# An encoder block on one core: four transposes move between the first products, attention scores start one step sooner, pooling uses four banks, and the operands of the last product lie at other addresses

## The chip, the core and the metric

The kernel runs on one core of a Trainium2 chip. The metric is the device time of one execution in microseconds. Five engines work in parallel, each in its own program order: TensorE (PE in the profile; its weight loads are PEld), VectorE (DVE), ScalarE (ACT), GpSimd (POOL) and SyncE (SP, which only issues transfers). Engines wait for one another through semaphores. Products accumulate in PSUM banks; everything else lies in SBUF, 128 partitions wide.

## The reference

```python
h = rmsnorm(x) * norm_gain
z = h @ w_in                     # 256 x 1024 by 1024 x 8192
a_in, a_gate, q, k, v, b_gp, g_logits = split(z)
y_a = (pooled_means(a_in) @ w_pool * pool_scale * silu(a_gate)) @ w_proj_a
att = dilated_attention(q, k, v) # 3 groups x 8 heads of 64, biased, masked;
                                 # the groups share one softmax denominator
y_b = (att * silu(b_gp)) @ w_proj_b
merged = sigmoid(gA) * y_a + sigmoid(gB) * y_b
return rmsnorm(x + merged @ w_out) * final_gain
```

There are 256 tokens, two blocks of 128. `pooled_means` takes centred means over 2, 4, 8 and 16 tokens, minus the token.

## The kernel before

**Three products for one.** Each float32 operand is split into a rounded high part and the rest. A product is then three matmuls, high by high, high by low and low by high, which `mm3` records (L249, L250, L251). `hh` and `hl` are the parts of the normalised input, `whi` and `wlo` those of a weight tile. One half of a weight tile, 128 output channels by 256 tokens, is 8 x 3 = 24 matmuls of 256 columns.

**The head** (to 16 us) is ordered by hand, in `manual_schedule`, on ACT, DVE, PE and POOL. X is squared, summed and scaled into `XN`, one token block b at a time; DVE scales channels 0 to 511 and ACT channels 512 to 1023 (L196, L197). `turn(kc, b)` (L206) transposes channel block kc of token block b on PE into `tps[kc % 4]`: four PSUM banks, each holding channel blocks kc and kc + 4. ACT reads a turned block into `hh` (L225), and DVE makes `hl` from it (L226). `part0(kc, x)` (L215) records two products of the first weight tile: x = 0 is high by high, x = 1 takes `hl`, x = 2 takes `wlo`. DVE copies the first weight tile into `whi0` in two halves (L199), and POOL computes its low part (`cut_lo`, L165). Three small products for the bias lines (L239) stand between the x = 2 products.

**The stages** that follow are ordered by a scheduler from the program's text. They work through weight tiles: k, q and v of the first four head pairs (I = 0), then u, a and b (pool input and the two gates), then v, k and q of I = 1, then eight gate tiles g with the pooling product mx before the eighth, then the two projections y, and at last the product with `w_out`, whose accumulators are called both and out. While tile n is multiplied, tile n + 2 is split (`cut_half`, L129 on ACT, L134 on DVE).

**Attention items.** An item is a head pair hq and a token block b. `stage_s` makes its scores (four matmuls, sp, L294 and L296), DVE adds the bias and finds the row maximum (L297, L303), ACT exponentiates (L306). `stage_t` turns the result (pt, L318) and splits it (L320, L321). `stage_o` multiplies with v (op, L332 and L335); after the second token block of a pair, ACT and DVE add the result into `ATT` (L346 to L348). There is one score bank pair ("S") and one op bank ("O"). `step()` is called after every half tile. It records at most one op, one turning and one new score; an item is turned two steps after its scores, and multiplied two steps after that. `due` grows by `rate` at each step, and a new item starts when it passes 0.99.

**Addresses.** `skip(nbytes, name)` allocates a tile that nobody uses and so moves what is allocated after it. `MH` and `ML`, the parts of the merged result, take the places of the bias tile ("bias") and of the keys ("kl").

**Projection banks.** Accumulators of half tiles rotate through three banks ("mm").

Of the kernel before, what the change touches and what calls it, by code (L numbers as in the profile page):

```python
# [12 lines left out]
F32R = mybir.dt.float32r  # L13
# [4 lines left out]
P = 128  # L18
D = 1024
S = 256  # L20
KC = D // P
# [21 lines left out]
def encoder_block(ctx: ExitStack, tc: tile.TileContext, x, w_in, lines, w_pool, w_proj_a, w_proj_b,  # L43
                  w_out, final_gain, params, out):
    nc = tc.nc
# [7 lines left out]
    def slot(shape, dt, tag, name, bufs=1):  # L53
        return sb.tile(shape, dt, tag=tag, name=name, bufs=bufs)

    def skip(nbytes, name):

        if nbytes:
            sb.tile([P, nbytes // 4], F32, name=name)

    def bank(shape, tag, name, bufs):
        return ps.tile(shape, F32, tag=tag, name=name, bufs=bufs)

    def mmb(name, shape=(P, S)):
        return bank(list(shape), "mm", name, 3)
# [97 lines left out]
    def cut_lo(n, k0, k1, eng):  # L163
        t, (hi, lo) = raws[n][0], parts[n]
        return eng.tensor_tensor(lo[:, k0:k1, :], t[:, k0:k1, :], hi[:, k0:k1, :].bitcast(F32), op=ALU.subtract)  # L165
# [6 lines left out]
    with tc.manual_schedule(engines={mybir.EngineType.Activation, mybir.EngineType.DVE, mybir.EngineType.PE,  # L172
                                    mybir.EngineType.Pool}):
        tiny = sb.tile([P, 1], F32, name="tiny")
        warm = sb.tile([P, P], F32, name="warm")
        nc.vector.memset(warm, 0.0)
        nc.scalar.activation(tiny, warm[:, 0:1], AF.Square)

        def keep_warm(times):
            for _ in range(times):  # L180
                nc.tensor.matmul(misc[:, P:2 * P], warm, warm, start=True, stop=True)

        keep_warm(WARM)
        halves = [slice(h * 512, (h + 1) * 512) for h in range(2)]
        for b in range(2):
            sq = [slot([P, 512], F32, "st", f"sq{b}{h}", 3) for h in range(2)]
            nc.scalar.activation(sq[0], X[:, b, halves[0]], AF.Square, scale=1.0 / 32.0, accum_out=ss[:, b, 0:1])
            xb = X[:, b, halves[1]]
            nc.vector.tensor_tensor_reduce(sq[1], xb, xb, scale=1.0 / D, scalar=EPS, op0=ALU.mult, op1=ALU.add,
                                           accum_out=ss[:, b, 1:2])  # L190
            t = slot([P, 1], F32, "rt", f"rt{b}", 2)
            nc.vector.tensor_tensor(t, ss[:, b, 0:1], ss[:, b, 1:2], op=ALU.add)
            nc.gpsimd.tensor_tensor(rs[:, b:b + 1], t, mhalf, op=ALU.pow)
        open_parts(0)
        for b in range(2):
            nc.vector.tensor_scalar(XN[:, b, halves[0]], X[:, b, halves[0]], rs[:, b:b + 1], None, op0=ALU.mult)  # L196
            nc.scalar.activation(XN[:, b, halves[1]], X[:, b, halves[1]], AF.Copy, scale=rs[:, b:b + 1])  # L197
        for k in (0, 4):
            nc.vector.tensor_copy(parts[0][0][:, k:k + 4, :], raws[0][0][:, k:k + 4, :])  # L199

        cut_lo(0, 0, 5, nc.gpsimd)
        first_lo = cut_lo(0, 5, 8, nc.gpsimd)
        tps = [bank([P, 2, S], "mm" if i < 3 else "T", f"tp{i}", 3 if i < 3 else 2) for i in range(4)]

        def turn(kc, b):
            nc.tensor.transpose(tps[kc % 4][:, kc // 4, b * P:(b + 1) * P], XN[:, b, kc * P:(kc + 1) * P], ident)  # L206

        acc = bank([P, 2, 512], "S", "k00", 1)
        acc0 = [acc[:, u, 0:S] for u in range(2)]

        def part0(kc, x):
            hi_, lo_ = parts[0]
            for u in range(2):
                c = slice(u * P, (u + 1) * P)
                nc.tensor.matmul(acc0[u], (lo_ if x == 2 else hi_)[:, kc, c], (hl if x == 1 else hh)[:, kc, :],  # L215
                                 start=x == 0 and kc == 0, stop=x == 2 and kc == KC - 1)

        for kc in range(KC):
            turn(kc, 0)
        for kc in range(KC):  # L220
            turn(kc // 2 + kc % 2 * 4, 1)
        for kc in range(KC):
            v = tps[kc % 4][:, kc // 4]
            gcol = prm[:, kc:kc + 1]
            nc.scalar.activation(hh[:, kc, :], v, AF.Copy, scale=gcol)  # L225
            nc.vector.scalar_tensor_tensor(hl[:, kc, :], v, gcol, hh[:, kc, :].bitcast(F32), op0=ALU.mult,  # L226
                                           op1=ALU.subtract)
            part0(kc, 0)
            if kc >= 2:
                part0(kc - 2, 1)  # L230
        for kc in (6, 7):
            part0(kc, 1)
        for kc in range(KC):
            if kc == 5:

                for t in range(3):
                    w = 3 * NH
                    o = 3 * P + t // 2 * w
                    nc.tensor.matmul(misc[:, t * w:(t + 1) * w], oh[:, t * P:(t + 1) * P], oh[:, o:o + w],  # L239
                                     start=True, stop=True)  # L240
            part0(kc, 2)
        cut_next()
        nc.vector.tensor_copy(line.rearrange("p i r h -> p r i h"),
                              misc[:, 0:LROW * NH].rearrange("p (r i h) -> p r i h", i=2, h=4))
        cut_next()
    parts.pop(0)

    def mm3(acc, ah, al, bh, bl, first, last):
        nc.tensor.matmul(acc, ah, bh, start=first, stop=False)  # L249
        nc.tensor.matmul(acc, ah, bl, start=False, stop=False)  # L250
        nc.tensor.matmul(acc, al, bh, start=False, stop=last)  # L251
# [101 lines left out]
    due, rate = [1.0 - RATES[0]], [RATES[0]]  # L353

    def step():
        clock[0] += 1
        for it in live:
            if it["at"] == "t" and it["when"] <= clock[0]:
                stage_o(*it["it"], it["p"])
                it["at"] = "done"  # L360
                break
        live[:] = [it for it in live if it["at"] != "done"]
        for it in live:
            if it["at"] == "s" and it["when"] <= clock[0]:
                it["p"] = stage_t(*it["it"], it["st"])
                it["at"], it["when"] = "t", clock[0] + LAG_O
                break
        due[0] = due[0] + rate[0] if wait else due[0]
        if wait and due[0] > 0.99:
            due[0] -= 1.0  # L370
            it = wait.pop(0)
            live.append({"it": it, "at": "s", "when": clock[0] + LAG_T, "st": stage_s(*it)})
# [95 lines left out]
    def bias(I):  # L468
        T = skew.pop(I)
        t = slot([P, S + 4 * 640], F32, "bias", f"BT{I}")  # L470
        BL[I], BT[I] = t[:, 0:S], t[:, S:].rearrange("p (h c) -> p h c", c=640)
        by = T.rearrange("p c a h -> p h a c")
        for h in range(4):
            nc.gpsimd.tensor_copy(BT[I][:, h, 0:384].rearrange("p (a c) -> p a c", c=64), by[:, h, 0:6])
        for rl in range(2):
            rows = slice(rl * 64, (rl + 1) * 64)
            for g in range(2):
                o = 384 + g * P + 64 * (rl if g == 0 else 1 - rl)
                nc.gpsimd.tensor_copy(BT[I][rows, :, o:o + 64], by[rows, :, 6 + g + rl])
                o = 384 + g * P + 64 * (1 - rl if g == 0 else rl)  # L480
                behind(nc.gpsimd.memset(BT[I][rows, :, o:o + 64], MASK), first_lo)
# [6 lines left out]
    heads(0, "k")  # L488

    heads(0, "q")  # L490
    bias(0)
    U = sb.tile([P, 4, UW], F32, tag="uu", name="U")
    nc.gpsimd.memset(U[:, :, 0:PAD], 0.0)
    nc.gpsimd.memset(U[:, :, PAD + S:], 0.0)
    heads(0, "v")
    skip(608, "pt")
    wait += [(0, hq, b) for hq in range(4) for b in range(2)]


    for dst in ("u", "a", "b"):  # L500
# [15 lines left out]
    for g, w in enumerate(POOL_W):  # L516
        h = w // 2
        cur, lo_, n_ = U[:, g, :], 0, UW
        k = 1
# [36 lines left out]
    heads(1, "q")  # L556
    bias(1)
    rate[0] = RATES[1]
    due[0] = 1.0 - rate[0]
    wait += [(1, hq, b) for hq in range(4) for b in range(2)]  # L560


# [32 lines left out]
    AML = slot([P, 4, S], F32R, "t4", "AML")  # L595
    wph, wpl = weights(n)
    n += 1
    for g in range(4):
        acc = mmb(f"mx{g}") if g < 3 else bank([P, 2, 512], "S", "mx3", 1)[:, 0, 0:S]
        mm3(acc, wph[:, g, :], wpl[:, g, :], PH[:, g, :], PL[:, g, :], True, True)  # L600
        am = AM[:, g, :].rearrange("p (r j) -> p r j", r=4)
        nc.vector.scalar_tensor_tensor(am, acc.rearrange("p (j r) -> p r j", r=4), prm[:, 24 + g:25 + g],
                                       SA[:, g, :].rearrange("p (r j) -> p r j", r=4), op0=ALU.mult,
                                       op1=ALU.mult)
# [47 lines left out]
    squash((GG[:, 8:12], G2))  # L652

    MH = slot([P, 8, S], F32R, "bias", "MH")
    ML = slot([P, 8 * S + 32], F32R, "kl", "ML")[:, 32:].rearrange("p (c j) -> p c j", j=S)

    def done_b(cb, acc):
        nc.vector.tensor_tensor(GB[cb], acc, GB[cb], op=ALU.mult)
# [183 lines left out]
```

## Time and profile before

| | |
|---|---|
| time, median of 3 runs | 260.26 us (259.99 to 260.36) |
| the profiled execution | 260.05 us, of which the span from first to last instruction is 258.3 us |
| granted TensorE clock, mean | 0.993 |
| PE busy | 250.5 us, 97% of the span |
| DVE, ACT, POOL busy | 209.4, 164.6 and 76.6 us |
| first transpose; first product of the head | 7.21 us; 9.27 us |
| first product of the second weight tile | 16.00 us |
| q of I = 0; v of I = 0; u | from 26.9; 43.2; 59.5 us |
| g; both and out; last matmul starts | from 152.8; 229.37; 251.87 us |

The page gives busy time, but matmuls are pipelined, so a busy PE can still issue at different distances. The start times of matmuls show this, and so do the durations that the trace notes for them. Times are from the span's start. The names in a row are output<-inputs. A row with "idle before <-" names what ended the idle time of that engine.

### The profile page before, as it was taken

The numbers are of one execution on the slowest core, as the hardware profiler recorded it, in microseconds if no ns is written. First come the engines' busy times: TensorE is split into PE (matmuls) and PEld (weight loads), VectorE is DVE, ScalarE is ACT, GpSimd is POOL, SyncE is SP. The second block draws the span as 40 slices with busy tenths as digits, with TensorE's granted clock in tenths as the row PEclk, the third lists the DMA queues.
The fourth block names the chain that finished last, engine by engine and source line by source line (L and its number), as shares of the span: only waits on it lengthen the run. The fifth ranks groups of instructions, "written<-read, shape, count | busy, mean of one in ns | idle before, by whom it ended". The sixth has DMA issues, their size and how long they took to land.

```text
span 258.3 us, 5483 instructions
## 1 busy us (share of the span) xinstructions
PE 250.5 (97%) x2160; PEld 249.1 (96%) x2160; DVE 209.4 (81%) x408; ACT 164.6 (64%) x286; POOL 76.6 (30%) x105
## 2 busy tenths in 40 slices
PE   8999999999999999999999999999999999999990
PEld 8899999999999999999999999999999999999990
DVE  2899979778888787889697997967849998899383
ACT  4878577565666565658967778655549994446140
POOL 1562419201798000010671950000210030442011
PEclk9999999999999999999999999999999999999997
DMA  6998999996444644454899897144440598300022
GB/s 232 385 414 325 275 258 326 302 323 241 166 162 162 246 162 166 162 165 162 261 259 210 287 249 302 46 165 162 160 167 0 179 371 291 141 3 1 3 81 81
DMA packets 9992, 52.01 MB, mean 201 GB/s; under 512 B 1147, under 2 KB 2142, under 8 KB 4718
## 3 DMA queue, kind: packets, MB, share of 16 engines
q1 hardware_dynamic: 7022, 44.08, 49.6%
q0 software_dynamic: 2512, 7.12, 11.2%
q10 hardware_dynamic: 432, 0.46, 0.5%
q8 instruction: 17, 0.28, 0.4%
q14 instruction: 9, 0.07, 0.1%
HBM read 47.42 MB, written 1.09 MB: 188 GB/s over the span
## 4 chain that ended last, share of the span: by engine, by line
PE 86%; DVE 6%; issue 3%; DMA 2%; ACT 1%; POOLq 0%; POOL 0%; SPq 0%; DVEq 0%; ACTq 0%
PE v L249 4%; PE v L251 4%; PE v L250 4%; PE q L251 4%; PE q L249 4%; PE q L250 4%; PE g L249 4%; PE g L251 4%; PE g L250 4%; PE k L249 4%; PE k L251 4%; PE k L250 4%; PE y L249 3%; PE y L251 3%; PE y L250 3%
## 5 line engine op out<-in xcount | busy, mean ns | idle before, releaser
L134 DVE TENSOR_TENSOR wlo<-wraw,whi 128x512 fp32r<-128x512 f32 (+1 forms) x130 | 107.5, 865 | 8.3 <-ACT whi L129 7.4
L129 ACT ACTIVATE whi<-wraw 128x1024 fp32r<-128x1024 f32 (+1 forms) x80 | 81.0, 1038 | 22.7 <-PE q L250 10.1
L249 PE MATMUL g<-hh,whi 128*128 128x256 f32 x128 | 35.8, 279 | 0.0
L251 PE MATMUL g<-hh,wlo 128*128 128x256 f32 x128 | 35.4, 276 | 0.0
L250 PE MATMUL g<-hl,whi 128*128 128x256 f32 x128 | 35.3, 276 | 0.0
L306 ACT ACTIVATE st<-st,nm 128x512 f32<-128x512 f32 x16 | 11.6, 724 | 28.7 <-DVE nm L303 28.7
L249 PE MATMUL v<-whi,hh 128*128 128x256 f32 x96 | 26.6, 277 | 0.0
L251 PE MATMUL v<-whi,hl 128*128 128x256 f32 x96 | 26.5, 276 | 0.0
L250 PE MATMUL v<-wlo,hh 128*128 128x256 f32 x96 | 26.5, 276 | 0.0
L251 PE MATMUL q<-hh,wlo 128*128 128x256 f32 x96 | 26.5, 276 | 0.0
L249 PE MATMUL q<-hh,whi 128*128 128x256 f32 x96 | 26.5, 276 | 0.0
L250 PE MATMUL q<-hl,whi 128*128 128x256 f32 x96 | 26.5, 276 | 0.0
L249 PEld LDWEIGHTS g<-hh,whi 128*128 128x128 f32 x128 | 24.0, 188 | 0.1
L250 PEld LDWEIGHTS g<-hl,whi 128*128 128x128 f32 x128 | 24.0, 188 | 0.0
L251 PEld LDWEIGHTS g<-hh,wlo 128*128 128x128 f32 x128 | 24.0, 188 | 0.0
L249 PE MATMUL k<-hh,whi 128*128 128x256 f32 x80 | 22.2, 277 | 0.0
L251 PE MATMUL k<-hh,wlo 128*128 128x256 f32 x80 | 22.1, 277 | 0.0
L250 PE MATMUL k<-hl,whi 128*128 128x256 f32 x80 | 22.1, 277 | 0.0
L250 PEld LDWEIGHTS v<-wlo,hh 128*128 128x128 f32 x96 | 18.0, 188 | 0.0
L250 PEld LDWEIGHTS q<-hl,whi 128*128 128x128 f32 x96 | 18.0, 188 | 0.0
L251 PEld LDWEIGHTS q<-hh,wlo 128*128 128x128 f32 x96 | 18.0, 188 | 0.0
L249 PEld LDWEIGHTS q<-hh,whi 128*128 128x128 f32 x96 | 18.0, 188 | 0.0
(179 smaller groups left out, 764.1 us busy)
## 6 DMA issues: line engine op xcount, KB each, us to landing
wraw<-in_w_in_dram SPq DMA_DIRECT2D x31, 1024.0 KB, 6.6
wraw<-in_w_out_dram SPq DMA_DIRECT2D x4, 1024.0 KB, 5.6
T<-line_d POOLq DMA_DIRECT2D x4, 576.0 KB, 8.7
KX<-KX POOLq DMA_DIRECT2D x8, 256.0 KB, 17.2
wraw<-in_w_proj_a_dram SPq DMA_DIRECT2D x2, 1024.0 KB, 4.9
wraw<-in_w_proj_b_dram SPq DMA_DIRECT2D x2, 1024.0 KB, 4.9
X<-in_x_dram SPq DMA_DIRECT2D x2, 512.0 KB, 4.2
wraw<-in_w_in_dram SPq DMA_DIRECT2D x2, 512.0 KB, 6.6
```

The costliest lines, as they stand in the source:

```text
L129: nc.scalar.activation(hi[:, s, :], t[:, s, :], AF.Copy)
L134: (nc.gpsimd if kind == "pool" else nc.vector).tensor_tensor(lo[:, s, :], t[:, s, :], hi[:, s, :].bitcast(F32), op=ALU.subtract)
L249: nc.tensor.matmul(acc, ah, bh, start=first, stop=False)
L250: nc.tensor.matmul(acc, ah, bl, start=False, stop=False)
L251: nc.tensor.matmul(acc, al, bh, start=False, stop=last)
L306: e = nc.scalar.activation(st, st, AF.Exp, bias=nm, scale=-1.0, accum_out=l)
```

## The change

Five places change.

1. *Head.* Of the second token block, only channel blocks 0 to 3 are turned ahead of the products. Blocks 4 to 7 are turned between them, each after the products that take `hl` of the block in the other half of its bank. DVE's copy of the second half of `whi0` (`copy0(4)`) moves behind the first `hl`.
2. *First scores.* One more `step()` is called between v and u, so that the first item starts there and every item of I = 0 one step sooner.
3. *Item pattern.* `due` starts I = 1 at 0.666 instead of 0.333. New items then start at steps 1, 2, 4, 5, 7, 8, 10 and 11 of the stage, before at 1, 3, 4, 6, 7, 9, 10 and 12.
4. *Pooling banks.* The four accumulators of mx take two "mm" banks and both halves of "S", before three "mm" banks and one half; all four products are written ahead of the four reads.
5. *Addresses.* Of the 608 skipped bytes, 384 move ahead of the bias tile, and `ML` starts 128 bytes earlier in its slot. As built, `MH` starts 64 bytes past a multiple of 256, before 192; so does `ML`, before 192 as well. `hh`, `hl`, `PHL`, `AMH` and `ATHL` start at 64 past such a multiple, `whi` and `wlo` at 128, before and after.

```diff
--- before.py
+++ after.py
@@ -195,11 +195,10 @@
         for b in range(2):
             nc.vector.tensor_scalar(XN[:, b, halves[0]], X[:, b, halves[0]], rs[:, b:b + 1], None, op0=ALU.mult)
             nc.scalar.activation(XN[:, b, halves[1]], X[:, b, halves[1]], AF.Copy, scale=rs[:, b:b + 1])
-        for k in (0, 4):
+        def copy0(k):
             nc.vector.tensor_copy(parts[0][0][:, k:k + 4, :], raws[0][0][:, k:k + 4, :])

-        cut_lo(0, 0, 5, nc.gpsimd)
-        first_lo = cut_lo(0, 5, 8, nc.gpsimd)
+        copy0(0)
         tps = [bank([P, 2, S], "mm" if i < 3 else "T", f"tp{i}", 3 if i < 3 else 2) for i in range(4)]

         def turn(kc, b):
@@ -215,19 +214,33 @@
                 nc.tensor.matmul(acc0[u], (lo_ if x == 2 else hi_)[:, kc, c], (hl if x == 1 else hh)[:, kc, :],
                                  start=x == 0 and kc == 0, stop=x == 2 and kc == KC - 1)

-        for kc in range(KC):
-            turn(kc, 0)
-        for kc in range(KC):
-            turn(kc // 2 + kc % 2 * 4, 1)
-        for kc in range(KC):
+        def split_h(kc):
             v = tps[kc % 4][:, kc // 4]
             gcol = prm[:, kc:kc + 1]
             nc.scalar.activation(hh[:, kc, :], v, AF.Copy, scale=gcol)
             nc.vector.scalar_tensor_tensor(hl[:, kc, :], v, gcol, hh[:, kc, :].bitcast(F32), op0=ALU.mult,
                                            op1=ALU.subtract)
+
+        for kc in range(KC):
+            turn(kc, 0)
+        for kc in range(4):
+            turn(kc, 1)
+        split_h(0)
+        copy0(4)
+
+        cut_lo(0, 0, 5, nc.gpsimd)
+        first_lo = cut_lo(0, 5, 8, nc.gpsimd)
+        part0(0, 0)
+
+        for kc in range(1, KC):
+            split_h(kc)
             part0(kc, 0)
-            if kc >= 2:
-                part0(kc - 2, 1)
+            if kc == 1:
+                turn(4, 1)
+            if kc != 2:
+                part0(max(kc - 2, 0), 1)
+            if 3 <= kc <= 5:
+                turn(kc + 2, 1)
         for kc in (6, 7):
             part0(kc, 1)
         for kc in range(KC):
@@ -488,13 +501,16 @@
     heads(0, "k")

     heads(0, "q")
+    skip(384, "pb")
     bias(0)
     U = sb.tile([P, 4, UW], F32, tag="uu", name="U")
     nc.gpsimd.memset(U[:, :, 0:PAD], 0.0)
     nc.gpsimd.memset(U[:, :, PAD + S:], 0.0)
     heads(0, "v")
-    skip(608, "pt")
+    skip(224, "pt")
     wait += [(0, hq, b) for hq in range(4) for b in range(2)]
+
+    step()


     for dst in ("u", "a", "b"):
@@ -556,7 +572,8 @@
     heads(1, "q")
     bias(1)
     rate[0] = RATES[1]
-    due[0] = 1.0 - rate[0]
+
+    due[0] = 2.0 * (1.0 - rate[0])
     wait += [(1, hq, b) for hq in range(4) for b in range(2)]


@@ -595,9 +612,13 @@
     AML = slot([P, 4, S], F32R, "t4", "AML")
     wph, wpl = weights(n)
     n += 1
+
+    pair = bank([P, 2, 512], "S", "mx2", 1)
+    mx = [mmb("mx0"), mmb("mx1"), pair[:, 0, 0:S], pair[:, 1, 0:S]]
     for g in range(4):
-        acc = mmb(f"mx{g}") if g < 3 else bank([P, 2, 512], "S", "mx3", 1)[:, 0, 0:S]
-        mm3(acc, wph[:, g, :], wpl[:, g, :], PH[:, g, :], PL[:, g, :], True, True)
+        mm3(mx[g], wph[:, g, :], wpl[:, g, :], PH[:, g, :], PL[:, g, :], True, True)
+    for g in range(4):
+        acc = mx[g]
         am = AM[:, g, :].rearrange("p (r j) -> p r j", r=4)
         nc.vector.scalar_tensor_tensor(am, acc.rearrange("p (j r) -> p r j", r=4), prm[:, 24 + g:25 + g],
                                        SA[:, g, :].rearrange("p (r j) -> p r j", r=4), op0=ALU.mult,
@@ -652,7 +673,7 @@
     squash((GG[:, 8:12], G2))

     MH = slot([P, 8, S], F32R, "bias", "MH")
-    ML = slot([P, 8 * S + 32], F32R, "kl", "ML")[:, 32:].rearrange("p (c j) -> p c j", j=S)
+    ML = slot([P, 8 * S + 32], F32R, "kl", "ML")[:, 0:8 * S].rearrange("p (c j) -> p c j", j=S)

     def done_b(cb, acc):
         nc.vector.tensor_tensor(GB[cb], acc, GB[cb], op=ALU.mult)
```

`part0` and `mm3` are unchanged. In the changed program lines lie further down (L215 becomes L214, L249 to L251 become L262 to L264). The new order shows at three places.

PE in the head, after the eight transposes of the first token block (tp is a bank of `tps`, k the accumulator of the first tile). Before:

```order
L206 MATMUL tp_138<-ident,XN 128x128 x2
L206 MATMUL tp_139<-ident,XN 128x128 x2
L206 MATMUL tp_140<-ident,XN 128x128 x2
L206 MATMUL tp_141<-ident,XN 128x128 x2
L215 MATMUL k_142<-hh,whi_128 128x256 x6
L215 MATMUL k_142<-hl,whi_128 128x256 x2
L215 MATMUL k_142<-hh,whi_128 128x256 x2
```

Now, from the transpose of channel block 3:

```order
L205 MATMUL tp_138<-ident,XN 128x128
L214 MATMUL k_139<-hh,whi_128 128x256 x4
L205 MATMUL tp_135<-ident,XN 128x128
L214 MATMUL k_139<-hl,whi_128 128x256 x2
L214 MATMUL k_139<-hh,whi_128 128x256 x4
L214 MATMUL k_139<-hl,whi_128 128x256 x2
L205 MATMUL tp_136<-ident,XN 128x128
L214 MATMUL k_139<-hh,whi_128 128x256 x2
L214 MATMUL k_139<-hl,whi_128 128x256 x2
L205 MATMUL tp_137<-ident,XN 128x128
L214 MATMUL k_139<-hh,whi_128 128x256 x2
L214 MATMUL k_139<-hl,whi_128 128x256 x2
```

Four transposes stand ahead of the first product instead of eight; the other four (the fourth comes after the rows shown) each stand between pairs of products.

DVE in the head, from the scaling of X on. Before:

```order
L196 TENSOR_SCALAR XN<-X,rs 128x512 x2
L199 CAST whi_128<-wraw_76 128x1024 x2
L226 SCALAR_TENSOR_TENSOR hl<-tp_138,prm,hh 128x256
L226 SCALAR_TENSOR_TENSOR hl<-tp_139,prm,hh 128x256
L226 SCALAR_TENSOR_TENSOR hl<-tp_140,prm,hh 128x256
```

Now:

```order
L196 TENSOR_SCALAR XN<-X,rs 128x512 x2
L199 CAST whi_128<-wraw_76 128x1024
L221 SCALAR_TENSOR_TENSOR hl<-tp_135,prm,hh 128x256
L199 CAST whi_128<-wraw_76 128x1024
L221 SCALAR_TENSOR_TENSOR hl<-tp_136,prm,hh 128x256
L221 SCALAR_TENSOR_TENSOR hl<-tp_137,prm,hh 128x256
```

The second copy stands behind the first `hl` instead of ahead of it.

PE at the end of v and the start of u, now (before, the u rows follow the v rows directly, and the sp rows stand behind the 24 matmuls of u's first half):

```order
L264 MATMUL v_784<-whi_645,hl 128x256
L307 MATMUL sp_817<-KX_254,QS_252 128x2x128 x2
L309 MATMUL sp_817<-K_255,QS_252 128x256 x2
L262 MATMUL u_832<-hh,whi_709 128x256
L263 MATMUL u_832<-hl,whi_709 128x256
```

The first scores, which read the keys, now stand ahead of u.

## The prediction

> **What bounds the kernel now.** I read the page first, then PE's waits, then the distance between matmuls stage by stage.
>
> ```profile
> span 258.3 us, 5483 instructions
> PE 250.5 (97%) x2160; PEld 249.1 (96%) x2160; DVE 209.4 (81%) x408; ACT 164.6 (64%) x286; POOL 76.6 (30%) x105
> PE   8999999999999999999999999999999999999990
> ```
>
> ```profile
> PE misc L181 <- DVE warm L176: 1.1, 1, 1.1
> PE tp L206 <- DVE XN L196: 0.4, 1, 0.4
> PE op L332 <- DVE ATT L348: 0.2, 1, 0.2
> ```
>
> PE is busy from the head to the end, and past the head its waits show one entry, of 0.2 us. So a microsecond more or less of PE's stream is a microsecond of the kernel. Time can be won only where PE waits in small pieces, or where matmuls follow one another at a longer distance. That distance is not the same everywhere. The next rows (PE's instructions on a tile: shortest, median and longest duration in ns, first and last start) show it; the last two are single matmuls, the first and the last of the product with `w_out`.
>
> ```profile
> L249 PE MATMUL q<-hh,whi x48: 276/276/276, 26.9 to 42.9; 128*128 128x256 f32 x48
> L251 PE MATMUL q<-hh,wlo x48: 276/276/277, 27.1 to 43.1; 128*128 128x256 f32 x48
> L249 PE MATMUL v<-whi,hh x48: 276/276/277, 43.2 to 59.2; 128*128 128x256 f32 x48
> ...
> L249 PE MATMUL u<-hh,whi x24: 281/281/283, 59.5 to 68.1; 128*128 128x256 f32 x24
> L251 PE MATMUL u<-hh,wlo x24: 281/281/282, 59.8 to 68.4; 128*128 128x256 f32 x24
> ...
> L249 PE MATMUL a<-hh,whi x15: 281/281/281, 75.9 to 80.9; 128*128 128x256 f32 x15
> ...
> L249 PE MATMUL v<-whi,hh x8: 279/279/363, 115.6 to 118.2; 128*128 128x256 f32 x8
> ...
> L249 PE MATMUL k<-hh,whi x8: 279/281/281, 118.5 to 121.0; 128*128 128x256 f32 x8
> ...
> L249 PE MATMUL out<-whi,MH x48: 281/281/281, 232.2 to 251.6; 128*128 128x256 f32 x48
> ...
> 229.37 0.28 PE L249 MATMUL both<-whi,MH 128*128 128x256 f32 x1
> ...
> 251.87 0.28 PE L251 MATMUL out<-whi,ML 128*128 128x256 f32 x1
> ```
>
> q has 144 matmuls from 26.9 to 43.1 us: 16.2 us over 143 distances, 113.3 ns. The last product has 192 from 229.37 to 251.87 us: 22.5 us over 191 distances, 117.8 ns. The durations mark the two: 276 ns in q and v, 281 ns in the last product, in u up to 68.4 us, in part of a, and near it around 118 us, where v gives way to k. I call them the quick and the slow distance; they are 4.5 ns apart. PE streams at the slow one for about 75 matmuls of u and its scores (59.5 to 68.4 us), 52 around a (75.6 to 81.7 us), 47 around v and k (115.8 to 121.4 us) and 191 at the end. That is 365 x 4.5 ns = 1.64 us.
>
> **The change part by part.** *Head.* Rows of the head before:
>
> ```profile
> 8.15 0.56 PE L206 MATMUL tp<-ident,XN 128*128 128x128 f32 x2
> 8.74 3.18 ACT L225 ACTIVATE hh<-tp,prm 128x256 fp32r<-128x256 f32 x8 [0.42 <-PE tp L206]
> 9.16 0.69 DVE L199 CAST whi<-wraw 128x1024 fp32r<-128x1024 f32 x1 [0.46 <-DMA wraw<-in_w_in_dram]
> 9.27 0.87 PE L215 MATMUL k<-hh,whi 128*128 128x256 f32 x4
> 9.77 3.22 DVE L226 SCALAR_TENSOR_TENSOR hl<-tp,prm,hh 128x256 fp32r<-128x256 f32 x8
> 9.93 4.78 POOL L165 TENSOR_TENSOR wlo<-wraw,whi 128x1280 fp32r<-128x1280 f32 x2 [2.36 <-DVE whi L199]
> ...
> 13.46 1.34 PE L215 MATMUL k<-hh,wlo 128*128 128x256 f32 x10
> ...
> 15.23 0.93 PE L215 MATMUL k<-hh,wlo 128*128 128x256 f32 x6
> ...
> L225 ACT ACTIVATE hh<-tp,prm 128x256 fp32r<-128x256 f32 x8 | 3.2, 476 | 0.4 <-PE tp L206 0.4
> L206 PE MATMUL tp<-ident,XN 128*128 128x128 f32 x16 | 2.1, 283 | 0.4 <-DVE XN L196 0.4
> ```
>
> The pair of transposes that starts at 8.15 ends at 8.71; ACT starts the first `hh` at 8.74, it ends 0.47 us later, and the product starts at 9.27. So from a transpose's start (8.71 - 0.28 = 8.43) to the product that takes it pass some 0.86 us. In the change the first `hh` needs only the first of the pair, about 0.23 us earlier: the first product starts at 9.04. That is the gain. What is lost: blocks 4 to 7 now run this loop of 0.86 us while products wait for it. Between the transpose of block 5 and the first product of block 5, PE has that transpose, four products and the next transpose, 0.11 + 4 x 0.113 + 0.11 = 0.67 us, and waits 0.19 us. For block 7 there are only the transpose and four products, 0.56 us, and it waits 0.30 us; block 6 is covered by the wait of block 5. A matmul after a wait has a distance of about 0.2 us instead of 0.11 (four products in 9.27 + 0.87 have (0.87 - 0.28) / 3 = 0.20): 0.1 us more at each wait. The first two pairs are paced by ACT as before (0.14 us and the 0.1 twice), and the third pair waits for the second `hl` behind DVE's copy (0.1 us). So the 32 products of x = 0 and 1 and the four transposes take 32 x 0.113 + 4 x 0.11 = 4.06 us plus 0.34 + 0.10 + 0.29 + 0.40 = 1.13 us: the x = 2 products start at 14.2 us instead of 13.46. Cost: 0.75 us. Bounds: if only the first two pairs wait, 9.04 + 4.06 + 0.34 = 13.44, nothing; if blocks 5, 6 and 7 all wait like block 7, 3 x 0.40 in place of 0.69, it is 1.25. Each part of the loop has its row, so I take 0.75. POOL's second low part ended at 14.71 and now ends 0.25 us later, as DVE's second copy does; the last x = 2 products, at 15.23 before and 15.97 now, still come after it.
>
> *First scores.* Their four matmuls only move. They read keys that POOL's queue copies late:
>
> ```profile
> L442 POOL DMA_DIRECT2D KX<-KX x4: 590/631/672, 26.6 to 31.3; - x4
> DMA to landing us min/median/max: 23.8/27.1/28.9
> ```
>
> The last copy lands at 31.3 + 28.9 = 60.2 us at the latest; the scores now come at 59.5 + 0.75 = 60.25, not after another 24 x 0.118 = 2.8 us. The first item needs the earlier copies only, so 0; if it waited for the last, and that one 0.3 us later through the later head, 0.3. Behind it in PE's order stands u. For the distance, the slow one began where v met u, and each later switch lies at an item's matmuls. All those places shift by a half tile. I cannot say which will be slow, so I take half of the 174 slow matmuls of u, a, v and k: 87 x 4.5 ns, a gain of 0.4 us (bounds 0.8 gained, none).
>
> *Item pattern.* The one wait past the head:
>
> ```profile
> 188.26 0.28 PE L251 MATMUL g<-hh,wlo 128*128 128x256 f32 x1
> 188.71 0.47 PE L332 MATMUL op<-pp,VS 128*128 128x256 f32 x2 [0.17 <-DVE ATT L348]
> ```
>
> The first op of a pair waits until DVE has read the pair before from the one op bank. Before, one half tile (24 x 0.113 = 2.7 us) lies between them; with the new steps two do. The distance of 0.45 us becomes 0.11, and the 0.08 after it (the same 0.2 as above) goes too: gain 0.4 us. What is late next is DVE's queue, 81% busy over the span; it gets the same work in nearly the same steps, and its splits run a tile ahead. One group of item matmuls more stands alone: 0.05 us lost. Bounds: 0.4 gained, 0.4 lost if the wait only moves to another pair.
>
> *Pooling banks.* PE at mx:
>
> ```profile
> 200.32 0.28 PE L251 MATMUL mx<-PHL,wlo 128*128 128x256 f32 x1
> 200.55 0.38 PE L249 MATMUL mx<-PHL,whi 128*128 128x256 f32 x1
> 200.77 0.28 PE L250 MATMUL mx<-PHL,whi 128*128 128x256 f32 x1
> ...
> 201.24 0.28 PE L251 MATMUL mx<-PHL,wlo 128*128 128x256 f32 x1
> 201.44 0.38 PE L249 MATMUL g<-hh,whi 128*128 128x256 f32 x1
> 201.66 0.28 PE L250 MATMUL g<-hl,whi 128*128 128x256 f32 x1
> ```
>
> Four distances of 0.23, 0.22, 0.20 and 0.22 us stand where 0.113 would do: the third accumulator waits for a bank that ACT still reads, the next gate tile for one that DVE reads. The score banks have been free since DVE read the last scores, so both waits go: 0.4 us gained, 0 if the gate tile still waits.
>
> *Addresses.* Nothing is added. Every stage with the quick distance pairs an operand at 64 past a multiple of 256 with one at 128; v does so with the same roles as the last product, weights moving and tokens stationary. Only the last product has 192. With `MH` and `ML` at 64 I expect v's 276 ns: 191 x 4.5 ns = 0.85 us gained. Bounds: 0 and 0.85.
>
> *Sum:* + 0.75 - 0.4 - 0.4 + 0.05 - 0.4 - 0.85 = -1.25 us. The profiled execution took 260.05 us, 0.21 under the median of the runs shown; 258.8 there is 259.0 as a median. A difference under 0.2%, 0.5 us, is no change here.
>
> **Rivals.** *Addresses change nothing.* For it: u, a and v switch distance with their addresses unchanged, so history alone can set it. Against it: the last product is slow throughout, 191 matmuls without a switch, and alone has 192. Then 259.0 + 0.85 = 259.85 us. [...]
>
> *The slow distance takes the long first stretch (slower than before).* From 16.0 to 59.4 us no item disturbs PE, and some 383 matmuls of k, q and v ran quick. If the distance goes by history alone, the head decides it, and the head changes. Slow there costs 383 x 4.5 ns = 1.7 us, and by the same mechanism the last product stays slow: 259.0 + 1.7 + 0.85 = 261.55 us. It outweighs the sum from 280 more slow matmuls on (1.25 us / 4.5 ns). Against it: the three small bias products and the x = 2 products just ahead of that stretch keep their order, and before they ended in the quick distance.
>
> *The head is free.* If the loop of 0.86 us is shorter than the rows suggest, the x = 2 products start at 13.4: 259.0 - 0.75 = 258.25 us. Against it: the rows of the loop.
>
> **How the numbers follow.** The forecast, 259.0, own range 258.4 to 259.6: chance 0.5. The head free, 258.25: 0.15. Addresses idle, 259.85: 0.2. History, 261.55: 0.1. The rest, 0.05, is a wait that only moved, near 260. For the range of 8 in 10 I go from 258.0, below the free head, to 260.5. Under 259.74 lie the first two and a third of the address rival, less a little for their upper tails: faster 0.67. Within 0.5 us of 260.26 the rest of it and the moved wait: 0.21. Slower 0.12.
>
> **What would show it.** Head: x = 2 products start near 14.2 us, with waits of PE at the products of blocks 5 and 7. Addresses: the median duration at the last product 276 instead of 281 ns. Pattern: no wait of op on DVE's `ATT`. Banks: all distances in mx near 0.11 us. First scores: near 60.25 us, without a wait for a copy. The prediction is wrong if k, q and v of the first stretch show 281 ns, if the x = 2 products start before 13.6 us, or if a new wait over 0.4 us stands in g.

## The result: slower, by a part that was counted as a gain

The changed kernel takes 267.69 us, the median of six executions from 264.08 to 268.85; the kernel before took 259.98 beside it (259.85 to 260.36, six executions). The ratio is 1.0248, with a 95% interval from 1.0212 to 1.0284: slower, where a gain had been forecast. The spread is part of the result: the profiled execution, 264.08 us with a span of 262.3, is the quickest of the six and ran at a mean granted clock of 0.995; the two longest ran at 0.980. Every ratio leaves out executions more than 1.5% above the quickest of their kernel, here 268.85 and 268.80 us and further down three single ones, which have no profile and are left out of the times given too: 362.52 us at a mean clock of 0.66 (copies later), 266.65 us at 0.95 (head alone) and 265.30 us (banks and addresses).

PE's waits in the changed kernel (engine, line, tile, what it waited for: us in all, times, longest):

```profile
...
PE pt L331 <- DVE st L325: 0.7, 2, 0.5
PE q L262 <- DVE KX L443: 0.4, 1, 0.4
PE k L214 <- ACT hh L220: 0.2, 1, 0.2
```

The wait of op on ATT is gone, as intended. Three new ones stand there: the transposes of the scores (pt) wait twice for DVE, and the first q product of the second half waits for DVE's evacuation of KX. These rows count the time in which PE had nothing at all to finish. Measured from start to start of the matmuls, the three places cost 0.73, 0.43 and 0.59 us, and a smaller one of the first kind near 100.7 us 0.16.

DVE in the changed kernel, ahead of the first pt wait, and PE's row that waits (start, us, engine, line, operation):

```profile
77.94 0.72 DVE L322 TENSOR_TENSOR st<-st 128x128 f32<-128x128 f32 x1
78.59 0.15 DVE L324 RECIPROCAL rl<-l 128x1 f32<-128x1 f32 x1
78.66 1.12 DVE L134 TENSOR_TENSOR wlo<-wraw,whi 128x512 fp32r<-128x512 f32 x1
79.70 0.78 DVE L325 TENSOR_SCALAR st<-st,rl 128x384 f32<-128x384 f32 x1
...
80.63 0.52 PE L331 MATMUL pt<-ident,st 128*128 128x128 f32 x3 [0.52 <-DVE st L325]
```

A weight split (L134) stands between the reciprocal and the scaling that needs it. It and the addition ahead of it are also long: at 113.27 us the same addition takes 0.29 us, and at 114.46 a split of this shape 0.69. POOL is busy with the window sums there (78.59 to 81.08).

Before, the same three operations stood side by side, and the transposes that need them came 1.5 us behind:

```profile
79.28 0.35 DVE L309 TENSOR_TENSOR st<-st 128x128 f32<-128x128 f32 x1 [0.88 <-ACT st L306]
79.55 0.15 DVE L311 RECIPROCAL rl<-l 128x1 f32<-128x1 f32 x1
79.74 0.79 DVE L312 TENSOR_SCALAR st<-st,rl 128x384 f32<-128x384 f32 x1
...
82.00 0.30 PE L318 MATMUL pt<-ident,st 128*128 128x128 f32 x1
```

PE's transposes came 1.37 us earlier with the change, but the end of the chain on DVE only 0.05 us (80.53 and 80.48): what the earlier start had won went into the split between and the longer addition. The order on DVE is new. Its program around the first item, in short, before and now:

```
before                                     now
st <- add of sums                          wlo split x2
rl <- reciprocal                           st <- add of sums
st <- scale                                rl <- reciprocal
wlo split x4                               wlo split
                                           st <- scale
```

Before, all eight items of the first half have their three short operations side by side; now, six of the eight have something between the reciprocal and the scale.

The third wait. DVE and POOL of the changed kernel around it:

```profile
132.02 1.23 DVE L134 TENSOR_TENSOR wlo<-wraw,whi 128x1024 fp32r<-128x1024 f32 x1
133.28 0.85 DVE L443 TENSOR_TENSOR KX<-k,KX 64x256 fp32r<-64x256 f32 x2
134.17 3.04 DVE L134 TENSOR_TENSOR wlo<-wraw,whi 128x1024 fp32r<-128x1024 f32 x1
137.24 0.87 DVE L443 TENSOR_TENSOR KX<-k,KX 64x256 fp32r<-64x256 f32 x2
...
133.17 1.30 POOL L568 TENSOR_TENSOR SB<-SB,sgsb 128x512 f32<-128x512 f32 x1
134.40 4.38 POOL L487 COPY BT<-T 128x384 f32<-128x384 f32 x4
```

One split of 1024 columns takes 1.23 us at 132.02 and 3.04 us at 134.17, while POOL copies the bias table of the second half. KX waits behind it on DVE, and the first q product needs the bank that KX still reads. Before, those copies began at 140.91 us, when KX was done, and the split in this place took 1.23 us:

```profile
134.17 1.23 DVE L134 TENSOR_TENSOR wlo<-wraw,whi 128x1024 fp32r<-128x1024 f32 x1
...
140.91 3.87 POOL L474 COPY BT<-T 128x384 f32<-128x384 f32 x4 [5.64 <-DMA T<-line_d]
```

POOL's order there, in short, before and now:

```
before                         now
DMA  T <- line_d               DMA  T <- line_d x2
SA <- SA,sgsa x2               SA <- SA,sgsa x2
DMA  K <- K x2                 SB <- SB,sgsb
SB <- SB,sgsb x2               DMA  K <- K x2
DMA  T <- line_d               SB <- SB,sgsb
DMA  KX <- KX x2               COPY BT <- T x8
COPY BT <- T x6                DMA  KX <- KX x2
DMA  KX <- KX x2               ATT <- ATT,SB x2
COPY BT <- T x2                DMA  KX <- KX x2
```

The scheduler sends for the table 10 us earlier (the second DMA was issued at 132.10 us before, and now with the first, from 121.58), and the copies start 6.5 us earlier. The first experiment below shows that the added step alone does this. The likely link is that the items of the first half now end earlier; no run isolates it.

The rest is distance between matmuls. From the third wait on, q of I = 1 and the start of g run at the slow distance, then y and the last product (shortest, median and longest duration in ns, first and last start):

```profile
L262 PE MATMUL q<-hh,whi x48: 281/281/356, 138.3 to 154.9; 128*128 128x256 f32 x48
...
L262 PE MATMUL g<-hh,whi x25: 281/281/369, 155.3 to 165.0; 128*128 128x256 f32 x25
...
L262 PE MATMUL y<-ATHL,whi x32: 281/281/281, 222.1 to 233.1; 128*128 128x256 f32 x32
```

The first and the last matmul of the product with `w_out`:

```profile
233.41 0.28 PE L262 MATMUL both<-whi,MH 128*128 128x256 f32 x1
...
255.90 0.28 PE L264 MATMUL out<-whi,ML 128*128 128x256 f32 x1
```

It again takes 22.5 us over 191 distances, 117.8 ns. In all, 808 of the matmuls of 256 columns start 117 to 120 ns after the one before them in this execution, and 418 before: 390 x 4.5 ns = 1.75 us. The profiled execution is 4.03 us over that of before: 0.8 at the head, 1.32 of pt's waits, 0.59 at q, 1.75 of distance, less 0.8 for op's wait and the pooling banks, 3.66. The remaining 0.4 us has no place. For the other five executions there is no profile of the changed kernel; the first experiment has one of the same kind.

### The profile page after: what moved, and what is told of

It is laid out like the page before. It is cut to its first block, busy times and chain, and to the rows that moved or that the text cites. A ratio compares the mean times of both kernels' runs of the same rounds, so it can differ in the third digit from the quotient of the medians.

```text
span 262.3 us, 5498 instructions
## 1 busy us (share of the span) xinstructions
PE 253.6 (97%) x2160; PEld 252.0 (96%) x2160; DVE 209.6 (80%) x408; ACT 165.7 (63%) x286; POOL 74.4 (28%) x105
## 4 chain that ended last, share of the span: by engine, by line
PE 88%; DVE 5%; issue 3%; ACT 1%; POOLq 0%; POOL 0%; DVEq 0%
PE g L262 6%; PE g L264 6%; PE g L263 6%; PE q L262 4%; PE q L264 4%; PE q L263 4%; PE k L262 4%; PE v L264 3%; PE v L263 3%; PE k L263 3%; PE v L262 3%; PE k L264 3%; PE y L262 3%; PE y L264 3%; PE y L263 3%
## 5 line engine op out<-in xcount | busy, mean ns | idle before, releaser
L134 DVE TENSOR_TENSOR wlo<-wraw,whi 128x512 fp32r<-128x512 f32 (+1 forms) x130 | 109.8, 870 | 17.9 <-ACT whi L129 16.9
L262 PE MATMUL g<-hh,whi 128*128 128x256 f32 x128 | 36.0, 281 | 0.0
L264 PE MATMUL g<-hh,wlo 128*128 128x256 f32 x128 | 35.5, 278 | 0.0
L262 PE MATMUL q<-hh,whi 128*128 128x256 f32 x96 | 26.8, 279 | 0.4 <-DVE KX L443 0.4
L264 PE MATMUL q<-hh,wlo 128*128 128x256 f32 x96 | 26.7, 279 | 0.0
L262 PE MATMUL v<-whi,hh 128*128 128x256 f32 x96 | 26.6, 277 | 0.0
L264 PE MATMUL v<-whi,hl 128*128 128x256 f32 x96 | 26.6, 277 | 0.0
L262 PEld LDWEIGHTS g<-hh,whi 128*128 128x128 f32 x128 | 24.1, 188 | 0.0
L264 PEld LDWEIGHTS g<-hh,wlo 128*128 128x128 f32 x128 | 24.1, 188 | 0.0
L262 PE MATMUL k<-hh,whi 128*128 128x256 f32 x80 | 22.2, 278 | 0.0
L264 PE MATMUL k<-hh,wlo 128*128 128x256 f32 x80 | 22.1, 276 | 0.0
L262 PEld LDWEIGHTS q<-hh,whi 128*128 128x128 f32 x96 | 18.0, 188 | 0.6 <-issue 0.6
L262 PEld LDWEIGHTS v<-whi,hh 128*128 128x128 f32 x96 | 18.0, 188 | 0.0
```

Of the source, the lines that this page charges most:

```text
L134: (nc.gpsimd if kind == "pool" else nc.vector).tensor_tensor(lo[:, s, :], t[:, s, :], hi[:, s, :].bitcast(F32), op=ALU.subtract)
```

## The experiments

In the expectations, theory S puts the loss on the place of the first scores, theory H on the head, theory D on the distance alone. Kernels of one group below ran beside the kernel before: 260.00 us for the first four, 259.94 for the next four, 260.02 for the last.

**First scores alone.** Before, with one line:

```
     wait += [(0, hq, b) for hq in range(4) for b in range(2)]
+    step()
```

> Before with the step of the first scores alone (first item work ahead of u). Theory S (the scores' place makes the loss: every item of the first half comes half a tile earlier against the evacuations on DVE and ACT, and the table copies of the second half come earlier on POOL): the waits of PE seen in the changed kernel stand here too, pt on DVE's st near 79 and 113 us (0.7 and 0.4 us) and the first q of the second half on DVE's KX near 137 us (0.6 us), and the time is 260.0 + 1.9 us of waits, 261.5 to 264 with the slow distance behind the last wait. Theory H (the head makes it, through a later start of all splits): 259.5 to 260.3, no such waits. Theory D (waits are small, the distance of 281 ns decides, by chance of history): somewhere in 259 to 263, by the count of slow matmuls.

267.42 us (265.07 to 268.28), ratio 1.0268 (1.0219 to 1.0317): the whole loss, without any of the other parts. The profiled execution is one of the long ones, 268.28 us with a clock of 0.979. Its waits; then PE, DVE and POOL in order of time; then by stretches the busy time of PE, PEld, DVE, ACT and POOL, the granted clock, DMA share and GB/s:

```profile
PE q L249 <- DVE KX L430: 3.0, 1, 3.0
...
PE pt L318 <- DVE st L312: 0.7, 2, 0.5
```

```profile
137.18 0.28 PE L251 MATMUL k<-hh,wlo 128*128 128x256 f32 x1
140.48 0.55 PE L249 MATMUL q<-hh,whi 128*128 128x256 f32 x1 [3.02 <-DVE KX L430]
...
146.36 0.28 PE L249 MATMUL q<-hh,whi 128*128 128x256 f32 x1
...
133.60 5.83 DVE L134 TENSOR_TENSOR wlo<-wraw,whi 128x1024 fp32r<-128x1024 f32 x1
139.46 0.88 DVE L430 TENSOR_TENSOR KX<-k,KX 64x256 fp32r<-64x256 f32 x2
...
133.84 3.37 POOL L474 COPY BT<-T 128x384 f32<-128x384 f32 x4
137.15 3.36 POOL L479 COPY BT<-T 64x256 f32<-64x256 f32 x4
```

```profile
137.50:139.00 1.50, 0.00 (x0) 0.00 (x0) 1.50 (x1) 1.46 (x3) 1.46 (x3) 1.00 0.56 182
139.00:140.50 1.50, 0.02 (x1) 0.05 (x1) 1.41 (x4) 1.29 (x2) 1.50 (x3) 0.66 0.01 5
140.50:145.00 4.50, 4.50 (x21) 4.50 (x22) 4.36 (x6) 0.00 (x0) 2.61 (x5) 0.50 0.66 148
145.00:146.40 1.40, 1.40 (x9) 1.40 (x9) 1.37 (x2) 0.41 (x2) 1.24 (x2) 0.53 1.15 374
146.40:150.00 3.60, 3.60 (x33) 3.60 (x33) 0.93 (x4) 1.48 (x3) 0.00 (x0) 1.00 1.24 277
```

The same split now takes 5.83 us, and PE stands still for 3.0 us. That idle time costs twice: during it the mean granted clock falls from 1.00 to 0.66, and from 140.5 until about 146.4 us it is 0.50 to 0.53. From 140.48 to 146.36 us 27 distances take 5.88 us instead of 3.06: 2.8 us. With 3.2 for the wait, 1.3 for pt and 0.9 for 202 more slow matmuls that is 8.2 us over 260.05, which is what this execution took. The copies delay the split by very different times in the two profiles, 3.04 and 5.83 us in all. That this also spreads the executions of the changed kernel is an inference: the mean clocks of its five others, 0.980 to 0.990, lie under that of the profiled one, but none of the five has a profile, and their times don't follow the clock throughout (266.36 us at 0.986, 267.70 at 0.990).

**All but the first scores.** The changed kernel without that line:

```
-    step()
```

> The changed kernel without the step of the first scores; head, item pattern, banks and addresses as in the change. Theory S: the three waits are gone; 260.0 + 0.8 (head) - 0.4 (op's wait) - 0.4 (banks), 259.2 to 260.2, the same in every execution. Theory H: still 263 to 268. Theory D: the waits are gone, and the time goes by the slow matmuls: each 100 of them 0.45 us.

260.66 us (259.73 to 261.12), ratio 1.0024 (1.0011 to 1.0036). All three waits are gone; PE's last entry is the 0.2 us of the first product. The times fall into two clusters, three from 259.73 to 259.98 and seven from 260.51 to 261.12. The expectation held for the first cluster only; what parts the two is taken up with the addresses.

**Head alone.** Before, with the new order of the head:

```
-        for kc in range(KC):
-            turn(kc // 2 + kc % 2 * 4, 1)
...
+            if 3 <= kc <= 5:
+                turn(kc + 2, 1)
```

> Before with the head's new order alone. Theory S: 260.0 + 0.8 = 260.8 us, x=2 products from 14.2 us, nothing else moved but the slow distances. Theory H: 263 us or more, and a mean granted clock below 0.99 in some executions as in the changed kernel. If the head is free: 260.0.

260.87 us (260.69 to 261.07), ratio 1.0030 (1.0020 to 1.0041). The head costs 0.87 us where 0.75 were forecast. Theory H is out: no time given for this kernel or the one without the first scores, which has the same head, reaches 263 us. The profile of the whole change shows the steps:

```profile
9.15 0.88 PE L214 MATMUL k<-hh,whi 128*128 128x256 f32 x4 [0.24 <-ACT hh L220]
...
11.84 0.50 PE L214 MATMUL k<-hh,whi 128*128 128x256 f32 x2
...
13.25 0.50 PE L214 MATMUL k<-hh,whi 128*128 128x256 f32 x2
...
14.28 1.30 PE L214 MATMUL k<-hh,wlo 128*128 128x256 f32 x10
```

The first product starts at 9.15 us, blocks 5 and 7 are waited for at 11.84 and 13.25, and the x = 2 products start at 14.28 (9.04 and 14.2 in the prediction). In the profile of the head alone they are 9.03 and 14.15.

**Item pattern alone.**

```
-    due[0] = 1.0 - rate[0]
+    due[0] = 2.0 * (1.0 - rate[0])
```

> Before with the item pattern of the second half alone. Theory S and the prediction: the wait of op on ATT near 188 us goes, 260.0 - 0.4 = 259.6 us. Theory H: the same. If the wait only moves: 260.0. Theory D: up to 1 us either way by the slow matmuls in y and out.

260.12 us (260.03 to 260.37), ratio 1.0007 (0.9997 to 1.0016): nothing that can be told. PE's waits past the head show one row:

```profile
...
PE mx L249 <- ACT G L575: 0.3, 1, 0.3
```

The wait of op went, and PE waits in its place at the third pooling accumulator, for a gate tile that ACT now reads later. With the new banks this wait goes too, but the sums below show no gain from the pattern there either.

**Copies later.** The changed kernel, with POOL's eight copies held behind its last key copy; PE, DVE, ACT and SP have the same order as in the change:

```
-                        nc.gpsimd.dma_start(t[oth], t[own])
+                        copied[0] = nc.gpsimd.dma_start(t[oth], t[own])
...
-            nc.gpsimd.tensor_copy(BT[I][:, h, 0:384]...
+            e = nc.gpsimd.tensor_copy(BT[I][:, h, 0:384]...
+            if I == 1:
+                behind(e, copied[0])
```

> The changed kernel, with POOL's eight copies of the second half's bias tables held behind its last key copy; PE, DVE, ACT and SP keep their orders word for word, only POOL's order moves. Theory P (POOL's copies starting during the split ahead of the KX evacuation hold DVE up, the first q then waits 0.6 to 3.3 us, and the clock drops when the wait is long): no wait of q on KX, that split 1.2 us instead of 3 to 6, granted clock at 0.992 or more in every execution, and 260.0 + 0.8 (head) + 1.2 (pt's waits on st, which stay) - 0.8 (op's wait, banks) = 261.2 us, up to 263 with slow distances. Rival Q (DVE's own queue is what is late at KX, POOL only coincides): the wait stays, and so do 264 to 268 us.

261.30, 261.45 and 262.10 us, ratio 1.0064 (1.0050 to 1.0079). Its DVE and POOL, and its waits:

```profile
133.87 1.40 DVE L134 TENSOR_TENSOR wlo<-wraw,whi 128x1024 fp32r<-128x1024 f32 x1
135.30 0.88 DVE L444 TENSOR_TENSOR KX<-k,KX 64x256 fp32r<-64x256 f32 x2
...
141.81 3.88 POOL L488 COPY BT<-T 128x384 f32<-128x384 f32 x4
```

```profile
PE pt L331 <- DVE st L325: 0.7, 2, 0.5
PE k L214 <- ACT hh L220: 0.2, 1, 0.2
```

One queue's order, and nothing else, takes the split from 3.04 us in the changed kernel to 1.40, removes q's wait, keeps the clock of the three executions at 0.994 to 0.998, and takes some 6 us off the time. The longest of the three, the profiled one, also has its last product at the slow distance, which is taken up with the addresses. This settles the third wait. How the copies hold the split up is not shown; measured are its times, 1.23 us before, ahead of POOL's copies, and 3.04 and 5.83 us beside them, and that it ended only within the third copy and the seventh (last section).

**Addresses alone.** The three lines of the change on paddings and `ML`; no engine's order changes:

```
+    skip(384, "pb")
...
-    skip(608, "pt")
+    skip(224, "pt")
...
-    ML = slot([P, 8 * S + 32], F32R, "kl", "ML")[:, 32:]...
+    ML = slot([P, 8 * S + 32], F32R, "kl", "ML")[:, 0:8 * S]...
```

> Before with the addresses alone; no engine's order changes. Theory A (addresses at 192 past a multiple of 256 hold the last product at the slow distance): out at 276 ns, 260.0 - 0.85 = 259.15 us. Theory D (history alone): out stays at 281 ns, 260.0. Mixed (the address permits the quick distance, the state on entry decides): two clusters, near 259.2 and near 260.0.

259.15 us (258.94 to 259.26), ratio 0.9968 (0.9956 to 0.9980). The last product in it:

```profile
L249 PE MATMUL out<-whi,MH x48: 276/276/277, 232.0 to 250.7; 128*128 128x256 f32 x48
```

That is the term of the prediction, 0.79 us for 0.85, and it refutes the rival by which addresses change nothing. This is also the quickest kernel whose executions agree.

**Banks alone.** `mx` on two banks of its own:

```
+    pair = bank([P, 2, 512], "S", "mx2", 1)
+    mx = [mmb("mx0"), mmb("mx1"), pair[:, 0, 0:S], pair[:, 1, 0:S]]
```

> Before with the pooling banks alone; no engine's order changes. By the prediction the four long distances in mx and behind it go, 260.0 - 0.4 = 259.6 us. If the gate tile behind it still waits, 260.0.

259.61 us (259.10 to 259.83), ratio 0.9984 (0.9975 to 0.9993): 0.33 us for 0.4. In the changed kernel the first matmuls of the four accumulators have a median of 278 ns:

```profile
L262 PE MATMUL mx<-PHL,whi x4: 276/278/333, 203.3 to 204.4; 128*128 128x256 f32 x4
```

**Pattern, banks and addresses**, the changed kernel without head and first scores:

> Before with item pattern, banks and addresses, without head and without first scores. The single terms of the prediction: -0.35, -0.4, -0.85: 258.4 us if out is quick, 259.2 if it is slow; if the pattern alone is worth nothing because its gain went into the wait of mx on ACT's G, the banks take that wait away too, and the sum stays. With theory D in two clusters 0.85 us apart.

Two clusters: seven executions from 258.95 to 259.27 us, five from 259.76 to 260.05; ratio 0.9981 (0.9971 to 0.9990). The profiled one, of the lower cluster, has the last product at 276 ns.

**Banks and addresses:**

> Before with banks and addresses alone, every engine's order as before. If the two gains measured one by one add up (0.33 and 0.79 us): 258.9 us, lower than every kernel so far. If the wait on the pooling banks is what pushes the last product into one distance or the other, two clusters, near 258.9 and 259.7.

Two clusters again: six from 258.67 to 259.23, five from 259.98 to 260.21; ratio 0.9981 (0.9968 to 0.9994). The lower cluster agrees with the sum of the two single gains, and its best is the best time of all; but with five executions in the upper one the kernel is no better than the addresses alone. Nothing in the program differs between executions, so the addresses allow the quick distance and don't secure it. Only the lower clusters were profiled. That the upper ones have the last product at 117.8 ns is an inference from the distance between the clusters: 0.88 us by the medians in the kernel with the pattern, which fits, and 1.18 us here, of which 0.85 would be explained. Besides the changed kernel's, one profile does show a last product that stayed slow with the addresses of the change, that of the copies later (262.10 us; its two other executions are 0.65 and 0.8 us quicker):

```profile
L262 PE MATMUL out<-whi,MH x48: 280/280/281, 234.2 to 253.7; 128*128 128x256 f32 x48
```

**No window sums.** The kernel with the copies later, without the ten POOL additions of the window sums, whose values are then missing from the output. The run asks whether these additions have a part in the two waits of pt:

```
-        while k < w:
+        while k < 1:
```

> The changed kernel with POOL's table copies later (as e5), and without the ten additions by which POOL builds the window sums from 65 to 81 us (their output is left out; PE, DVE, ACT and SP keep their orders). [...] Rival R (the new order on DVE, a split between the reciprocal and the scale of st, makes both waits by itself): both stay, 261.8 us.

260.72 and 261.92 us; copies later, with the additions, took 261.30 to 262.10. DVE at the place of the first pt wait, and PE's waits:

```profile
77.64 0.28 DVE L322 TENSOR_TENSOR st<-st 128x128 f32<-128x128 f32 x1
77.84 0.15 DVE L324 RECIPROCAL rl<-l 128x1 f32<-128x1 f32 x1
77.91 0.67 DVE L134 TENSOR_TENSOR wlo<-wraw,whi 128x512 fp32r<-128x512 f32 x1
78.50 0.41 DVE L325 TENSOR_SCALAR st<-st,rl 128x384 f32<-128x384 f32 x1
...
PE pt L331 <- DVE st L325: 0.2, 1, 0.2
```

The addition takes 0.28 instead of 0.72 us, the split 0.67 instead of 1.12, and the wait at 80 us is gone. So DVE's new order made the chain of one item longer, and POOL's additions made it too long. The additions alone don't: before, they ran beside this chain as well, and no wait of pt stands there. The wait near 113.5 us stays (0.44 us), where a piece of VS stands between the reciprocal and the scale. That it is the order which makes this one was not isolated by a run.

**One address at a time.** `MH` at 64 past a multiple of 256 and `ML` at 192, then the other way about:

> Before with MH's address alone at 64 past a multiple of 256 (ML stays at 192). If every matmul pays by the address it reads: the two thirds of the last product that read MH run at 276 ns, the third that reads ML at 281: 260.0 - 0.57 = 259.4 us. If one operand off 64 is enough for the slow distance throughout: 260.0. If one at 64 is enough for the quick one: 259.15.

> Before with ML's address alone at 64 past a multiple of 256 (MH stays at 192). If every matmul pays by the address it reads: 260.0 - 0.28 = 259.7 us. If one operand off 64 is enough for the slow distance: 260.0. If one at 64 is enough for the quick one: 259.15.

259.20 us (259.06 to 259.40, and one at 260.12), ratio 0.9976 (0.9964 to 0.9987), and 259.18 us (259.05 to 259.61), ratio 0.9971 (0.9959 to 0.9983). Both profiles show 276 ns in the last product from its sixth and fifth matmul on. One of the two operands moved is enough, so it isn't a price per matmul by the address that it reads.

The profiles of all fourteen kernels, read matmul by matmul (276 to 278 ns quick, 279 to 283 slow), say when the history counts:

| `MH`, `ML` | profiles | the last seven matmuls of y | the last product |
|---|---|---|---|
| 192, 192 | 5 | quick in 4, slow in 1 | slow from its second matmul at the latest, in all |
| 64, 64 | 7 | quick in 5, slow in 2 | quick in the same 5, slow in the same 2 |
| one of each | 2 | quick in 1, slow in 1 | quick from its sixth matmul at the latest, in both |

With both at 64 the last product kept the distance in which y ended, in all seven; the two slow ones are the changed kernel and the copies later. With both at 192 it went slow in all five, whatever came before. With one of each it went quick both times. Nothing here shows why.

## Why the prediction was wrong, point by point

- **First scores: the step that failed.** The prediction said "Their four matmuls only move" and credited the part with a gain of 0.4 us. The four matmuls did only move (they start at 60.30 us, 60.25 in the prediction). But the call is a step of the item clock, and every item of the first half moved with it. On DVE this put splits inside the items' short chains: 1.32 us of waits. On POOL it brought the second half's table copies ahead of the KX copies, and against the KX evacuations on DVE: 0.6 to 3.2 us of wait, and with the long one another 2.8 us through a granted clock of 0.50 to 0.53. Alone the part costs 7.4 us; with the copies held back, the two quicker executions show 1.5 us (261.30 and 261.45 against 259.87; the third has the slow last product). Both orders could be read from the program before any run, and the trace of before had the rows that price them: beside POOL's copies (from 140.91 us) a split of 512 columns took 1.14 us, and two took 1.29 where POOL for the most part issued key transfers instead (below). The prediction looked for waits on PE's own list and on the key copies, not at the queues whose order moved.

```profile
142.06 1.14 DVE L134 TENSOR_TENSOR wlo<-wraw,whi 128x512 fp32r<-128x512 f32 x1 [1.16 <-ACT whi L129]
...
147.27 1.29 DVE L134 TENSOR_TENSOR wlo<-wraw,whi 128x512 fp32r<-128x512 f32 x2
```

- **Head.** Right: 0.87 us for 0.75, and at the places named. The loop that it put at 0.86 us is 0.84 by its own rows (9.27 - 8.43), which changes little.
- **Item pattern.** Wrong: 0.35 us were to be gained, and none can be told (0.12 us lost, within the noise). The wait went as said; the sum then took the gain as kept, and it went into a wait on the pooling bank and some 58 more slow matmuls (476 for 418, 0.26 us). That rival, a wait that only moves, had been priced near 260.
- **Pooling banks.** Right: 0.33 us for 0.4.
- **Addresses.** Right alone, 0.79 us for 0.85, and worth nothing in the changed kernel, where y came to the slow distance ahead of the last product and the last product went on in it. The prediction took the address as sufficient. Its own rival, distance by history, describes what the changed kernel did, though not in the first stretch of k, q and v, which stayed quick, but in q, g, y and out.
- **The sum without first scores.** Head, pattern, banks and addresses as measured one by one are +0.87 + 0.12 - 0.33 - 0.79 = -0.13 us, 259.87. The lower cluster without the first scores stands there, 259.73 to 259.98, the same as before. So even without its worst part the change would have been no gain.
- **The rivals.** None of them had the mechanism: a queue off PE's path whose order moves. The rival on the slower side was priced at 261.55 us from distances, and no row was asked what an idle PE does to the granted clock.

## What to carry to other kernels

When an edit moves one step of a clock that other work follows, read the new order on every engine before pricing it, the queue that looks idle first: POOL, busy for 28% of the span, cost more here than all other parts together, through the operations of DVE that it delays. Ask of each new overlap of DVE and POOL which evacuation stands behind the delayed operation and which bank PE waits for. And price a wait of PE with what it does to the clock: with the first scores alone, 3.0 us of idle time was followed by 5.9 us at a granted clock of 0.50 to 0.53.

## What the runs showed of the hardware

- In the one long gap that was profiled, the idle PE lost its clock sooner than it got it back. In the profile of the first scores alone, the last k matmul ends at 137.46 us. The mean granted clock is 1.00 from 137.5 to 139.0 us, 0.66 from 139.0 to 140.5 and 0.50 from there to 145.0; if it fell at once, these means place the drop, as an estimate, near 139.5, 2.0 us after that end. Matmuls start again at 140.48, and full clock is back at 146.36, 5.9 us later.
- In two profiles POOL's copies in sequence held a DVE split off by more than one copy. In the changed kernel two copies of 0.89 us pass, the third takes 1.89, and the split ends within it after 3.04 us. With the first scores alone six copies of 0.62 to 0.89 us pass, the seventh takes 1.54, and the split ends within it after 5.83 us. In the kernel with the copies later, POOL's addition on ATT began during the same split; the split took 1.40 us, and the addition 1.73, where the next one took 0.73. In all three the split had started 0.23 to 0.26 us ahead of POOL's operation, so that start doesn't decide who goes first. What does was not found.
- The same program has two times 0.8 to 1.2 us apart, at the same granted clock, 0.992 to 0.998 in either cluster: with the addresses as in the change and the banks, or the banks and the pattern, beside them, five of eleven and five of twelve executions fell in the upper cluster. With the addresses alone all five were in the lower; with `MH` alone moved one of five was not. The table of profiles points to the distance in which the product before ends, but no upper cluster was profiled, and what sets that distance stays open. With the banks alone two of ten executions took 259.10 and 259.12 us and the others 259.57 or more; that is unexplained too.
